# One strided pattern of a dilated attention staged through a GpSimd copy

## The chip, the cores and the metric

The kernel runs on one core of one Trainium2 chip, as a single program. The metric is the device time of one execution in microseconds. Three timed runs of the kernel before gave 2363.19, 2372.0 and 2381.81 us; the median is 2372.0 us.

## The reference

The program is a two-layer decoder trunk over one sequence of 2048 positions of width 1024. The even layer (forgetting attention and gated linear attention) is not touched by the change. The odd layer runs two mixers in parallel on one input projection: a four-head retention and eight heads of dilated attention with 64 channels each. Queries and keys of both are rotated (rope): with the halves x1 and x2 of a head's channels, the result is x1 cos - x2 sin and x2 cos + x1 sin.

The dilated attention of a head is three causal window attentions, whose outputs are mixed by their softmax denominators. Pattern d (d = 1, 4, 16) takes the positions by residue modulo d, cuts every residue class into blocks of 128 and lets a block attend to itself and the block before it. With 2048 positions, dilation 1 has 16 blocks in one class, dilation 4 has 4 classes of 4 blocks, and dilation 16 has 16 classes of one block each, which attend to themselves alone.

```python
qs = to_strided(q)                 # (B, H, dil, nb, 128, dh)
kb = with_prev(to_strided(k))      # the block and the one before it
s = einsum('bhrnqd,bhrnkd->bhrnqk', qs, kb) * dh ** -0.5
p = exp(s - max(s));  den = sum(p)
o = einsum('bhrnqk,bhrnkd->bhrnqd', p, vb) / den;  lse = max(s) + log(den)
# out = sum over the three patterns of softmax(lse) * o
```

## The kernel before, in words

The kernel keeps float32 accuracy with pairs of float16 numbers: a high part and the rest. For each head of the dilated attention, `Heads.tiles` (L402) computes q, k and v for two tiles of 128 positions with 48 matmuls (L183 to L185), rotates q and k (`rope`, L1128, which calls `rotate`, L776: three VectorE multiplications and one GpSimd addition, L785), splits them (L425 to L434) and has them transposed by DMA (L440, SP queue) into `heads.st[h]`, a tile with 128 partitions, three planes (q; k high; k low) and 2048 positions in their natural order.

`dilated` (L869) attends. `groups` (L876) writes v to DRAM and reads it back in two strided orders (L878, L880, L882, all on GpSimd's queue), and forms 12 groups of four blocks each per head: groups 0 to 3 of pattern 0 (dilation 1), 4 to 7 of pattern 1 (dilation 4), 8 to 11 of pattern 2 (dilation 16). `scores` (L897) does the eight matmuls of a group, two for each block (q with k high, q with k low; L911, L912). The moving operand is a slice of `heads.st[h]` with step 1, 4 or 16: 256 columns where there is a block before, else 128; pattern 2 has only 128. VectorE then scales, masks and takes the maximum (L914), ScalarE exponentiates (L918) and makes the float16 high part (L920), VectorE the rest (L921), and two DMA transposes on the SP queue turn both (L922, L923, tile `dl_pt`). `values` (L926) multiplies them by v (L933, L934); ScalarE copies one half out of PSUM to `dl_o1` (L937), and VectorE adds the other half and writes the record `dl_rec` (L940, or L942 and L943). Records of patterns 1 and 2 go to DRAM and come back in natural order (L947, L948, GpSimd's queue). `mixed` (L950) combines the three records of a head.

The order is set in three places. `attend` (L978) lists the groups as 4 to 11 and then 0 to 3; `lagged` with LAG = 2 puts the values of a group behind the scores of the group two later; the last two values and `mixed` of a head go into the steps of the next head (`late`). `periods` (L448) and `merge` (L198) interleave these steps with other work: the tiles of the next head and the projections of the retention and the gate (`Extra.rows`, L240), each a unit with a cost in the plan. Before each step, `merge` issues as much of that work as the step's share of the plan's cost calls for; in the plan, scores cost 0.9 and values 0.7. Last, the framework's scheduler simulates the program and orders each engine's instructions by readiness, so that the order on an engine can differ from the order of the text.

After the eight heads, the retention (L789, which rotates with the same `rotate`) and the output projection of the odd layer (`mix_out`, L311) follow.

Of the kernel before, what the change touches and what calls it, by code (L numbers as in the profile page):

```python
# [7 lines left out]
F32 = mybir.dt.float32  # L8
F16 = mybir.dt.float16
BF16 = mybir.dt.bfloat16  # L10
I32 = mybir.dt.int32
AF = mybir.ActivationFunctionType
# [5 lines left out]
S = 2048  # L18
D = 1024
NT = 16  # L20
# [755 lines left out]
def rotate(co, work, x, cos, lo, hi, name):  # L776

    nc = co.nc
    r = work.tile(list(x.shape), F32, name=name)
    half = "p h (s d) -> p (h s) d" if len(x.shape) == 3 else "p j a (s d) -> p j (a s) d"  # L780
    nc.vector.tensor_mul(r.rearrange(half, s=2), x.rearrange(half, s=2), cos)
    y = work.tile(list(x.shape), F32, name=name + "_y", bufs=1)
    nc.vector.tensor_mul(y[..., 0:32], x[..., 32:64], lo)
    nc.vector.tensor_mul(y[..., 32:64], x[..., 0:32], hi)
    nc.gpsimd.tensor_add(r, r, y)  # L785
    return r


def retention(co, work, qkv_d, gn_w, gn_b, cst, rp):  # L789

    nc = co.nc
# [23 lines left out]
    def step(t, out):  # L815
# [4 lines left out]
        tabs = (rp[:, t, None, a:a + 32].to_broadcast([128, n, 32]) for a, n in ((0, 16), (32, 8), (64, 8)))  # L820
# [48 lines left out]
def dilated(co, work, keep, heads, cst, v_d, rec_d, mix_d):  # L869

    nc = co.nc
    mask = work.tile([128, 256], F32, name="dl_mask", bufs=1)
    nc.sync.dma_start(mask, cst["c_dmask"])
    recs, live = {}, {}

    def groups(h):  # L876
# [15 lines left out]
        for r0 in range(0, 16, 4):  # L892
            out.append((2, [(r, slice(r, S, 16), slice(r, S, 16), [v3[:, r, :]]) for r in range(r0, r0 + 4)]))
        recs[h] = [keep.tile([128, NT, 66], F32, name=f"dl_rec{i}", bufs=2 if i == 1 else 1) for i in range(3)]
        return out

    def scores(h, g, pat, units):  # L897
        rec, st, f = recs[h][pat], heads.st[h], heads.f[h]
        p = co.ps([128, 1024], "big")
# [6 lines left out]
        for n, qs, ks, vs in units:  # L906
            width = 128 * len(vs)
            sp = slice(at, at + width)
            spans.append(sp)
            at += width  # L910
            nc.tensor.matmul(p[:, sp], st[:, 0, qs], st[:, 1, ks], start=True, stop=False)  # L911
            nc.tensor.matmul(p[:, sp], st[:, 0, qs], st[:, 2, ks], start=False, stop=True)  # L912
# [13 lines left out]
    def values(h, g, pat, units):  # L926
# [9 lines left out]
        o1 = work.tile([128, 4, 64], F32, name="dl_o1", bufs=1)  # L936
        nc.scalar.activation(o1, pv[:, :, 0:64], AF.Copy)  # L937
        ns = [un[0] for un in units]
        if ns == sorted(ns):
            nc.vector.tensor_add(rec[:, ns[0]:ns[0] + 4, 0:64], pv[:, :, 64:128], o1)  # L940
        else:
            nc.vector.tensor_add(rec[:, 1:4, 0:64], pv[:, 0:3, 64:128], o1[:, 0:3, :])  # L942
            nc.vector.tensor_add(rec[:, 0:1, 0:64], pv[:, 3:4, 64:128], o1[:, 3:4, :])  # L943
# [34 lines left out]
    def attend(h, ready=None):  # L978
        gs = groups(h)
        order = [4, 5, 6, 7, 8, 9, 10, 11, 0, 1, 2, 3]  # L980
        steps = [(0.9, lambda g=g: scores(h, g, *gs[g]), 0.7, lambda g=g: values(h, g, *gs[g])) for g in order]
        units, wait = lagged(steps, LAG)
        for n, x in enumerate(late):
            units.insert(2 * n + 1, x)
        if ready:
            for i, x in enumerate(ready):
                units.insert(2 * len(late) + 1 + 5 * i, (0.0, x))
        late[:] = wait + [(0.0, lambda: mixed(h))]
        if ready:
            units += late  # L990
        return units
# [4 lines left out]
def decoder(tc, cst, x, norm_even, w_in_even, b_f_even, w_lr_even, b_lr_even, gla_norm_even, w_out_even,  # L996
            norm_odd, w_in_odd, ret_gn_w_odd, ret_gn_b_odd, w_out_odd, final_norm, out):
    nc = tc.nc
    with ExitStack() as ctx:
# [125 lines left out]
        rp = tab[1].tile([128, NT, 96], F32, name="rope")  # L1125
        nc.sync.dma_start(rp, cst["c_rope"])

        def rope(t, q):  # L1128
            tabs = (rp[:, t:t + 2, None, a:a + 32].to_broadcast([128, 2, n, 32])
                    for a, n in ((0, 4), (32, 2), (64, 2)))  # L1130
            return rotate(co, pre[1], q, *tabs, "dl_r")
# [53 lines left out]
def constants():  # L1185
# [17 lines left out]
    rope = np.concatenate([cos, -sin, sin], axis=1)  # L1203
    c["c_rope"] = rope.reshape(NT, 128, 96).transpose(1, 0, 2)
# [34 lines left out]
```

## Time and profile before

| | us |
|---|---|
| median of three runs (lowest, highest) | 2372.0 (2363.19, 2381.81) |
| the profiled execution, its own time | 2365.02 |
| its span, from the first instruction to the last | 2362.9 |
| TensorE matmuls busy | 2177.7 (92%) |
| VectorE busy | 1563.6 (66%) |
| ScalarE busy | 1123.3 (48%) |
| GpSimd busy | 520.9 (22%) |

The mean granted TensorE clock is 0.968 of full speed. Times in the trace are counted from the start of the span. The eight dilated heads run from about 1258 us (the first L911) to about 2064 us; before that lies the even layer, after it the retention and the last projection. PE is TensorE's matmul side, PEld its weight load, DVE VectorE, ACT ScalarE, POOL GpSimd, SP or SPq the queue of SyncE that issues the DMA transposes. Matmuls are pipelined: the time of one matmul in a row includes its way through the array, and the pace is read from the distance between the starts of neighbours.

### The profile page before, as it was taken

The page shows a single profiled execution, that of the slowest core. Times are in us where ns is not written, and L with a number is a line of the kernel's source. Part 1 is how long each engine was busy: PE and PEld are TensorE (multiplying, and loading weights), DVE is VectorE, ACT ScalarE, POOL GpSimd, SP SyncE. Part 2 cuts the span into 40 slices and gives each one's busy share as a digit, 9 for nine tenths or more (in the row PEclk, how much of TensorE's full clock was granted, in tenths as well). Part 3 has the DMA queues.
Part 4 walks back from the last instruction along what each step waited for, and adds up shares of the span by engine and source line. Part 5 has one row for each costly group of instructions (what it writes and reads, how often), then busy time and mean ns, then how long its engine had stood idle before and what let it go on. Part 6 is the DMA issues. An engine that isn't in the chain of part 4 may idle for free.

```text
span 2362.9 us, 51635 instructions
## 1 busy us (share of the span) xinstructions
PE 2177.7 (92%) x20020; PEld 1693.0 (72%) x20020; DVE 1563.6 (66%) x4878; ACT 1123.3 (48%) x2582; POOL 520.9 (22%) x638
## 2 busy tenths in 40 slices
PE   4978899998999999899999999999998899889998
PEld 3767787676688878654449988888887787755554
DVE  6556667575686667566557676757575757778764
ACT  5545455454554556344444554545454545533322
POOL 0021221211212111111112122231322122244431
PEclk7999999999999999999999999999999999989999
DMA  8658897988888858877876688786786668866553
GB/s 192 136 112 149 149 166 147 172 161 154 158 160 157 162 133 186 217 207 203 218 164 141 143 151 159 139 145 136 158 144 127 152 113 168 181 200 191 165 170 107
DMA packets 823606, 377.69 MB, mean 160 GB/s; under 512 B 726192, under 2 KB 782400, under 8 KB 823104
## 3 DMA queue, kind: packets, MB, share of 16 engines
q1 hardware_dynamic: 725936, 255.09, 55.9%
q0 software_dynamic: 23584, 82.33, 12.1%
q10 hardware_dynamic: 73840, 36.97, 6.4%
q8 instruction: 157, 2.57, 0.4%
q14 instruction: 89, 0.73, 0.1%
HBM read 135.40 MB, written 73.73 MB: 89 GB/s over the span
## 4 chain that ended last, share of the span: by engine, by line
PE 52%; DMA 21%; DVE 13%; issue 6%; ACT 5%; SPq 2%; POOL 1%; ACTq 0%; POOLq 0%; DVEq 0%
PE dn L183 9%; PE dn L185 9%; PE dn L184 9%; DMA dl_pt<-dl_pl 4%; DMA fx_tl<-fx_pl 4%; PE dn L354 3%; PE dn L356 3%; PE dn L355 3%; DMA o_gate<-gate_d 2%; PE big L911 2%; PE big L912 2%; PE aux L554 2%; PE big L522 2%; PE big L523 2%; DMA gl_x<-glq_d 1%
## 5 line engine op out<-in xcount | busy, mean ns | idle before, releaser
L183 PE MATMUL dn<-w,uh 128*128 128x192 f16 (+1 forms) x3840 | 1003.4, 261 | 14.7 <-DVE x_out L250 4.0
L184 PE MATMUL dn<-w,uh 128*128 128x192 f16 (+1 forms) x3840 | 1002.9, 261 | 0.0
L185 PE MATMUL dn<-w,ul 128*128 128x192 f16 (+1 forms) x3840 | 1002.3, 261 | 0.6 <-DMA ul<-u_lo 0.6
L183 PEld LDWEIGHTS <-uh 128*128 128x128 f16 x3968 | 391.6, 99 | 39.8 <-ACT uh L122 5.5
L184 PEld LDWEIGHTS <-uh 128*128 128x128 f16 x3968 | 390.6, 99 | 38.4 <-issue 11.0
L185 PEld LDWEIGHTS <-ul 128*128 128x128 f16 x3968 | 390.1, 99 | 28.8 <-DMA ul<-u_lo 2.8
L535 ACT ACTIVATE fx_s<-fx_s,fx_nm 128x1152 f32<-128x1152 f32 (+15 forms) x128 | 152.7, 1194 | 173.9 <-DVE fx_nm L533 170.8
L918 ACT ACTIVATE dl_s<-dl_s,dl_m 128x256 f32<-128x256 f32 (+1 forms) x384 | 172.7, 451 | 124.9 <-DVE dl_m L917 108.6
L540 DVE TENSOR_TENSOR fx_pl<-fx_s,fx_ph 128x2176 f16<-128x2176 f32 x64 | 155.2, 2424 | 93.5 <-DMA fx_tl<-fx_pl 59.2
L914 DVE CUSTOM_DVE_ANT_0 dl_s<-big,dl_mask,hd_f 128x256 f32<-128x256 f32 (+1 forms) x384 | 141.8, 421 | 52.9 <-PE big L912 51.7
L79 POOL TENSOR_TENSOR rs_r<-rs_v,mhalf 128x1 f32<-128x1 f32 (+2 forms) x96 | 68.1, 714 | 363.5 <-DVE rs_v L76 341.8
L527 DVE CUSTOM_DVE_ANT_0 fx_s<-big,cb,hd_f 128x1024 f32<-128x1024 f32 (+7 forms) x128 | 133.8, 1046 | 19.1 <-PE big L523 8.7
L921 DVE TENSOR_TENSOR dl_pl<-dl_s,dl_ph 128x512 f16<-128x512 f32 (+2 forms) x96 | 101.9, 1064 | 66.1 <-ACT dl_ph L920 38.3
L539 ACT ACTIVATE fx_ph<-fx_s 128x2176 f16<-128x2176 f32 x64 | 128.8, 2013 | 34.6 <-DMA fx_th<-fx_ph 31.1
L522 PE MATMUL big<-head 128*128 128x512 f16 (+3 forms) x320 | 112.9, 353 | 31.0 <-DVE fx_m L527 30.9
L84 ACT ACTIVATE w<-w_raw,w_gs 128x256 f16<-128x256 f32 (+2 forms) x296 | 113.7, 466 | 36.8 <-DVE w_gs L164 33.2
L911 PE MATMUL big<-head 128*128 128x256 f16 (+1 forms) x384 | 129.6, 355 | 0.9 <-DVE dl_rec L914 0.8
L912 PE MATMUL big<-head 128*128 128x256 f16 (+1 forms) x384 | 129.7, 357 | 0.0
L85 DVE SCALAR_TENSOR_TENSOR w<-w_raw,w_gs,w 128x256 f16<-128x256 f32 (+2 forms) x296 | 123.3, 469 | 8.4 <-ACT w L84 8.2
L555 PE MATMUL aux<-head,fx_tl 128*128 128x64 f16 x1088 | 102.3, 194 | 22.3 <-DMA fx_tl<-fx_pl 22.2
L566 POOL TENSOR_TENSOR fx_o<-fx_o 128x64 f32<-128x64 f32 x128 | 43.9, 362 | 343.1 <-DVE fx_o L560 212.3
L554 PE MATMUL aux<-head,fx_th 128*128 128x128 f16 x1088 | 107.2, 222 | 7.9 <-DMA fx_th<-fx_ph 7.9
(242 smaller groups left out, 4355.2 us busy)
## 6 DMA issues: line engine op xcount, KB each, us to landing
gate_d<-x_out POOLq DMA_DIRECT2D x64, 256.0 KB, 3.8
o_gate<-gate_d SPq DMA_DIRECT2D x32, 512.0 KB, 4.5
rec_d<-dl_rec POOLq DMA_DIRECT2D x16, 528.0 KB, 4.8
dl_rec<-rec_d POOLq DMA_DIRECT2D x16, 528.0 KB, 6.3
x_h<-in_x_dram SPq DMA_DIRECT2D x16, 512.0 KB, 4.8
cb<-cum_d SPq DMA_DIRECT2D x16, 512.0 KB, 9.7
o_mix<-mix_d SPq DMA_DIRECT2D x32, 256.0 KB, 2.8
o_h<-in_x_dram SPq DMA_DIRECT2D x16, 512.0 KB, 4.5
```

The source lines that it names most:

```text
L183: nc.tensor.matmul(out, uh[:, k, xs], wh[:, k, c0:c1], start=k == 0, stop=False)
L184: nc.tensor.matmul(out, uh[:, k, xs], wl[:, k, c0:c1], start=False, stop=False)
L185: self.last = nc.tensor.matmul(out, ul[:, k, xs], wh[:, k, c0:c1], start=False, stop=k == KT - 1)
L522: nc.tensor.matmul(p[:, k0:k1], q, st[:, ks, 1, 0:kn], start=True, stop=False)
L527: nc.vector.tensor_tensor_reduce(out=x[:, at + c * 1024:at + c * 1024 + wide], in0=p[:, :wide], in1=cb[c][:, :wide], scale=f[:, 0:1], scal ...
L535: nc.scalar.activation(x[:, sp], x[:, sp], AF.Exp, bias=nm[:, part:part + 1], accum_out=nm[:, 2 + part:3 + part])
L540: nc.vector.tensor_sub(pl, x[:, 0:W], ph)
L554: nc.tensor.matmul(pv[:, part, :], th[:, at, :], v[:, k, :], start=k == 0, stop=False)
L911: nc.tensor.matmul(p[:, sp], st[:, 0, qs], st[:, 1, ks], start=True, stop=False)
L912: nc.tensor.matmul(p[:, sp], st[:, 0, qs], st[:, 2, ks], start=False, stop=True)
L914: nc.vector.tensor_tensor_reduce(out=raw[:, sp], in0=p[:, sp], in1=mask[:, 256 - 128 * len(vs):], scale=f[:, 0:1], scalar=-3.0e38, op0=OP. ...
L918: nc.scalar.activation(raw[:, sp], raw[:, sp], AF.Exp, bias=m[:, i:i + 1], accum_out=rec[:, n, 65:66])
```

## The change

Four things change.

The operands of pattern 2 are copied. `stage(h, g)` lets GpSimd copy the 3 x 4 x 128 float16 values per partition that group g of pattern 2 needs from `heads.st[h]` (step 16 positions) into a contiguous tile `dl_g` with a single buffer. Group 8 is staged at the start of the scores of group 4, each next one right behind the matmuls of the group before it. The matmuls of pattern 2 read `dl_g`; those of patterns 0 and 1 read as before.

The groups are reordered to 4, 5, 8, 6, 9, 7, 10, 0, 11, 1, 2, 3, and the plan's costs become 1.05 and 0.84 (scores and values of patterns 0 and 1), 0.55 and 0.44 (pattern 2).

`values` no longer uses `dl_o1`: ScalarE writes into the record, and VectorE adds to it in place.

The rotary table holds cos and sin instead of cos, -sin and sin (64 columns instead of 96), and `rotate` replaces its one GpSimd addition by a subtraction on one half and an addition on the other, each of half the size.

```diff
-def rotate(co, work, x, cos, lo, hi, name):
+def rotate(co, work, x, cos, sin, name):
...
-    nc.vector.tensor_mul(y[..., 0:32], x[..., 32:64], lo)
-    nc.vector.tensor_mul(y[..., 32:64], x[..., 0:32], hi)
-    nc.gpsimd.tensor_add(r, r, y)
+    nc.vector.tensor_mul(y[..., 0:32], x[..., 32:64], sin)
+    nc.vector.tensor_mul(y[..., 32:64], x[..., 0:32], sin)
+    nc.gpsimd.tensor_sub(r[..., 0:32], r[..., 0:32], y[..., 0:32])
+    nc.gpsimd.tensor_add(r[..., 32:64], r[..., 32:64], y[..., 32:64])
...
-            out.append((2, [(r, slice(r, S, 16), slice(r, S, 16), [v3[:, r, :]]) for r in range(r0, r0 + 4)]))
+            out.append((2, [(r, None, None, [v3[:, r, :]]) for r in range(r0, r0 + 4)]))
...
+    def stage(h, g):
+
+        if g < 12:
+            staged[h, g] = work.tile([128, 3, 4, 128], F16, name="dl_g", bufs=1)
+            nc.gpsimd.tensor_copy(staged[h, g], heads.st[h].rearrange("p s (i r) -> p s r i", r=16)[:, :, 4 * (g - 8):4 * (g - 7), :])
+
     def scores(h, g, pat, units):
         rec, st, f = recs[h][pat], heads.st[h], heads.f[h]
+        if g == 4:
+            stage(h, 8)
...
-            nc.tensor.matmul(p[:, sp], st[:, 0, qs], st[:, 1, ks], start=True, stop=False)
-            nc.tensor.matmul(p[:, sp], st[:, 0, qs], st[:, 2, ks], start=False, stop=True)
+            q, kh, kl = ((st[:, 0, qs], st[:, 1, ks], st[:, 2, ks]) if pat < 2 else
+                         (staged[h, g][:, s, n % 4, :] for s in range(3)))
+            nc.tensor.matmul(p[:, sp], q, kh, start=True, stop=False)
+            nc.tensor.matmul(p[:, sp], q, kl, start=False, stop=True)
+        if pat == 2:
+            stage(h, g + 1)
...
-        o1 = work.tile([128, 4, 64], F32, name="dl_o1", bufs=1)
-        nc.scalar.activation(o1, pv[:, :, 0:64], AF.Copy)
         ns = [un[0] for un in units]
-        if ns == sorted(ns):
-            nc.vector.tensor_add(rec[:, ns[0]:ns[0] + 4, 0:64], pv[:, :, 64:128], o1)
-        else:
-            nc.vector.tensor_add(rec[:, 1:4, 0:64], pv[:, 0:3, 64:128], o1[:, 0:3, :])
-            nc.vector.tensor_add(rec[:, 0:1, 0:64], pv[:, 3:4, 64:128], o1[:, 3:4, :])
+        for a, b in ((0, 4),) if ns == sorted(ns) else ((0, 3), (3, 4)):
+            to = rec[:, ns[a]:ns[b - 1] + 1, 0:64]
+            nc.scalar.activation(to, pv[:, a:b, 0:64], AF.Copy)
+            nc.vector.tensor_add(to, pv[:, a:b, 64:128], to)
...
-        order = [4, 5, 6, 7, 8, 9, 10, 11, 0, 1, 2, 3]
-        steps = [(0.9, lambda g=g: scores(h, g, *gs[g]), 0.7, lambda g=g: values(h, g, *gs[g])) for g in order]
+        order = [4, 5, 8, 6, 9, 7, 10, 0, 11, 1, 2, 3]
+        steps = [(c, lambda g=g: scores(h, g, *gs[g]), 0.8 * c, lambda g=g: values(h, g, *gs[g]))
+                 for c, g in ((0.55 if g > 7 else 1.05, g) for g in order)]
...
-        rp = tab[1].tile([128, NT, 96], F32, name="rope")
+        rp = tab[1].tile([128, NT, 64], F32, name="rope")
...
-    rope = np.concatenate([cos, -sin, sin], axis=1)
-    c["c_rope"] = rope.reshape(NT, 128, 96).transpose(1, 0, 2)
+    rope = np.concatenate([cos, sin], axis=1)
+    c["c_rope"] = rope.reshape(NT, 128, 64).transpose(1, 0, 2)
```

## Rows read from the trace of the kernel before

**Rows 1.** The page's part 1: busy us, share of the span, instructions.

```profile
PE 2177.7 (92%) x20020; PEld 1693.0 (72%) x20020; DVE 1563.6 (66%) x4878; ACT 1123.3 (48%) x2582; POOL 520.9 (22%) x638
```

**Rows 2.** Stretches, dilated heads second: length, engines' busy us, clock, DMA share, GB/s.

```profile
0.00:1258.00 1258.00, 1136.04 (x10720) 863.30 (x10721) 807.38 (x2038) 611.17 (x1123) 210.44 (x329) 0.97 0.80 167
1258.00:2064.00 806.00, 763.86 (x7811) 675.58 (x7810) 544.90 (x2250) 417.53 (x1282) 194.82 (x209) 0.98 0.74 146
2064.00:2362.00 298.00, 277.81 (x1493) 154.13 (x1490) 211.31 (x591) 94.60 (x179) 115.59 (x102) 0.94 0.56 169
```

**Rows 3.** Waits of PE, 1258 to 2064 us: total us, times, longest.

```profile
PE aux L934 <- DMA dl_pt<-dl_pl: 29.3, 10, 6.8
PE aux L933 <- DMA dl_pt<-dl_ph: 9.5, 5, 4.9
```

**Rows 4.** Timeline of PE in a group of pattern 2: start, us, what.

```profile
1393.78 0.43 PE L912 MATMUL big<-head 128*128 128x128 f16 x1
1394.02 0.43 PE L911 MATMUL big<-head 128*128 128x128 f16 x1
1394.26 0.43 PE L912 MATMUL big<-head 128*128 128x128 f16 x1
```

**Rows 5.** Timeline of PE in a group of pattern 0, then values.

```profile
1438.44 0.27 PE L912 MATMUL big<-head 128*128 128x256 f16 x1
1438.55 0.22 PE L911 MATMUL big<-head 128*128 128x128 f16 x1
1438.60 0.22 PE L912 MATMUL big<-head 128*128 128x128 f16 x1
1438.66 0.22 PE L933 MATMUL aux<-dl_v,dl_pt 128*128 128x128 f16 x1
1438.72 0.19 PE L934 MATMUL aux<-dl_v,dl_pt 128*128 128x64 f16 x1
1438.74 0.22 PE L933 MATMUL aux<-dl_v,dl_pt 128*128 128x128 f16 x1
```

**Rows 6.** Groups on GpSimd, shapes apart, whole span: busy us, mean ns, idle before.

```profile
L785 POOL TENSOR_TENSOR dl_r<-dl_r,dl_r_y 128x256 f32<-128x256 f32 x64 | 50.9, 795 | 202.0 <-DVE dl_r_y L784 131.4 <-DVE w_tot L159 20.5 <-DVE w_am L153 18.6
L971 POOL TENSOR_TENSOR dl_rec<-dl_rec,dl_es 128x1024 f32<-128x1024 f32 x24 | 46.5, 1954 | 37.4 <-DVE dl_es L968 22.0 <-DVE dl_m L917 6.5 <-ACT dl_s L918 5.6
L501 POOL TENSOR_SCALAR cb<-cb,hd_f 128x1024 f32<-128x1024 f32 x16 | 45.5, 2843 | 81.0 <-DMA cb<-cum_d 81.0
```

**Rows 7.** Timeline of all engines at a head's start.

```profile
1364.46 5.89 SPq L440 DMA_TRANSPOSE head<-qk_x  x3
...
1370.39 0.28 PE L911 MATMUL big<-head 128*128 128x128 f16 x1
...
1371.45 0.55 POOL L882 DMA_DIRECT2D dl_v<-v_d  x1
```

**Rows 8.** DMA issues: size where shown, median us to landing.

```profile
head<-qk_x SPq DMA_TRANSPOSE x128, 4.2
```

**Rows 9.** Timeline of all engines while a head is mixed.

```profile
1899.00 5.62 POOL L971 TENSOR_TENSOR dl_rec<-dl_rec,dl_es 128x1024 f32<-128x1024 f32 x3 [7.01 <-DVE dl_es L968]
...
1902.80 2.91 DVE L972 TENSOR_TENSOR dl_rec<-dl_rec,dl_rec 128x1024 f32<-128x1024 f32 x1 [2.98 <-POOL dl_rec L971]
```

**Rows 10.** Groups on VectorE, shapes apart, 1258 to 2064 us.

```profile
L921 DVE TENSOR_TENSOR dl_pl<-dl_s,dl_ph 128x1024 f16<-128x1024 f32 x48 | 62.5, 1305 | 28.9 <-DMA dl_pt<-dl_pl 14.6 <-ACT dl_ph L920 12.8 <-ACT w L84 1.3
L972 DVE TENSOR_TENSOR dl_rec<-dl_rec,dl_rec 128x1024 f32<-128x1024 f32 x7 | 10.2, 1463 | 8.7 <-POOL dl_rec L971 8.7
```

**Rows 11.** Single lines of VectorE: ns min/median/max, first and last start.

```profile
L921 DVE TENSOR_TENSOR dl_pl<-dl_s,dl_ph x96: 678/1211/2795, 1275.5 to 2043.0; 128x1024 f16<-128x1024 f32 x48, 128x512 f16<-128x512 f32 x40, 128x896 f16<-128x896 f32 x8
L972 DVE TENSOR_TENSOR dl_rec<-dl_rec,dl_rec x8: 1214/1227/2908, 1385.5 to 2070.7; 128x1024 f32<-128x1024 f32 x8
```

**Rows 12.** Groups of the values, shapes apart, 1258 to 2064 us.

```profile
L937 ACT ACTIVATE dl_o<-aux 128x256 f32<-128x256 f32 x96 | 36.0, 376 | 69.5 <-PE aux L934 62.3 <-DVE dl_rec L940 6.3 <-DVE dl_rec L914 0.5
L940 DVE TENSOR_TENSOR dl_rec<-aux,dl_o 128x256 f32<-128x256 f32 x88 | 36.7, 417 | 20.6 <-ACT dl_o L937 20.5
```

More of the change, by code (lines that the diff above doesn't have):

```diff
@@ L819, in step @@
         v = z[:, 512:1024].rearrange("p (h n) -> p h n", n=128)
-        tabs = (rp[:, t, None, a:a + 32].to_broadcast([128, n, 32]) for a, n in ((0, 16), (32, 8), (64, 8)))
+        tabs = (rp[:, t, None, a:a + 32].to_broadcast([128, n, 32]) for a, n in ((0, 16), (32, 8)))
         r = rotate(co, work, z[:, 0:512].rearrange("p (h d) -> p h d", d=64), *tabs, "rt_r")
@@ L873, in dilated @@
     nc.sync.dma_start(mask, cst["c_dmask"])
-    recs, live = {}, {}
+    recs, live, staged = {}, {}, {}
     def groups(h):
@@ L1129, in rope @@
             tabs = (rp[:, t:t + 2, None, a:a + 32].to_broadcast([128, 2, n, 32])
-                    for a, n in ((0, 4), (32, 2), (64, 2)))
+                    for a, n in ((0, 4), (32, 2)))
             return rotate(co, pre[1], q, *tabs, "dl_r")
```

## The prediction

> **What bounds the kernel now.** I began with the page's busy shares: TensorE is busy for 92% of the span, VectorE for 66%, ScalarE for 48%, GpSimd for 22% [rows 1]. An average over the whole program says little about one stage, so I cut it at the dilated heads. Their stretch is 806 us long; TensorE is busy for 763.9 of it (95%) at a granted clock of 0.98, which is the higher of its two levels nearly all the time, VectorE for 544.9 (68%), ScalarE for 417.5 (52%), GpSimd for 194.8 (24%) [rows 2]. The reader is to see that TensorE alone sets the length there, and that GpSimd has the most room. TensorE's 42.1 us of idle time have nearly one cause: values that wait for their transposed probabilities, 29.3 + 9.5 us in 15 waits [rows 3]. In eight heads that is about two waits among twelve groups.
>
> **What the copies buy.** The pace of a matmul is the distance from its start to its neighbour's. In a group of pattern 2 the starts lie 0.24 us apart, for 128 columns read at a step of 16 positions [rows 4]. In a group of pattern 0, whose keys are contiguous, a matmul of 256 columns takes 0.11 us and one of 128 columns 0.05 to 0.06 us [rows 5]. The same 128 columns thus cost four times as much when they are read with a step. Staged operands are contiguous for q, k high and k low alike, so I take 0.057 us. Eight heads times four groups times eight matmuls are 256 matmuls; 256 x (0.24 - 0.057) = 46.8 us less on the engine that sets the end. Pattern 1 is not staged and keeps its pace. The bounds of this term are nothing (the pace came from something else than the step) and 256 x 0.19 = 48.6 us.
>
> **What the copies cost.** A copy moves 3 x 4 x 128 = 1536 values per partition; there are 32. No copy on GpSimd stands in the trace. The nearest row with one tensor operand is L501, 2.843 us for 1024 values, 2.8 ns each; the two-operand L971 takes 1.954 us for 1024, 1.9 ns each [rows 6]. That makes 2.9 to 4.3 us for a copy. I take 4.3, since L501 has the copy's single input; both rows read densely, so the step could make it longer, and TensorE's ratio of 0.24 to 0.057 gives the far end, 18 us. 32 x 4.3 = 138 us of GpSimd.
>
> [...]
>
> **Does TensorE wait for a copy?** The tile has one buffer, so the copy for the next narrow group starts after the matmuls of the one before. The plan's cost of a head is 12 steps: 1.8 x (8 x 1.05 + 4 x 0.55) = 19.08. TensorE's work of a head is 763.9 / 8 = 95 us, of which its own scores and values are some 25 us and the filling work 70 us (my count: 32 matmuls of 0.11, 32 of about 0.23, 32 of 0.24, 75 pairs of values of 0.085). Between two narrow scores lie two values, one wide score and the narrow one itself, 2.88 to 3.28 of 19.08, thus 10.6 to 12 us of filling and 2 to 3 us of its own: 12.5 to 15 us. A copy of 4.3 us leaves 8 us for delays in GpSimd's queue. The first copy of a head is tighter. It needs all transposes of q and k; in the second head these are issued from 1364.46 to 1370.35 us and land 4.2 us later, at about 1374.5, and on GpSimd it stands behind v's way through DRAM, whose last issue ends at 1372.0 [rows 7, 8]. Started at 1374.5, it ends near 1379. The head's first scores start at 1370.39 and its third group, now group 8, comes some 15 us later, near 1385: 6 us of slack. Behind a waiting copy stand GpSimd's stores of the projections, the rotations of the next head and the record transfers; they delay ScalarE's x_out buffers first. I allow 1 us for each of the eight first copies, 8 us (bounds 0 and 8 x 6).
>
> **What the copies do to VectorE.** While L971 ran from 1899.00 to 1904.62, L972 started at 1902.80 and took 2.91 us instead of its median of 1.227, ending 1.09 us after L971 did [rows 9, 11]. So a VectorE operation with two SBUF operands is held while GpSimd works. Over the stretch L921's wide form averages 1305 ns against a median of 1211, 4.5 us in 48, and L972 1463 against 1227, 1.7 us in 7 [rows 10, 11]; that is 6 us for 97 us of GpSimd arithmetic [rows 6]. If all of VectorE's 545 us stretched as these 73 us do, it would be 47 us. The added GpSimd work (138 us, and 26 us for the rotations below) then holds VectorE for 10 to 79 us; I take 25, near the low end, since most of its other operations read PSUM or one operand. VectorE has 261 us of idle time here, so only that part counts that makes a transpose late where TensorE waits already, 2 groups of 12: 4 us.
>
> [...]
>
> **The rest.** Each rotation's addition becomes two halves. From 795 ns for 256 and 1954 ns for 1024 values [rows 6] a half of 128 takes about 0.6 us, so two add 0.4 us: 26 us on GpSimd for 64 rotations, between VectorE and ScalarE work for the next head, hidden by TensorE's filling; without that cover 26 us more, and in the retention 16 x 0.4 = 6 us, also beside TensorE. The smaller table is one load, and nothing waits for it. Dropping `dl_o1` leaves 96 copies of 376 ns and 88 additions of 417 ns [rows 12] as they are, splits eight copies (at most 8 x 0.4 = 3 us of ScalarE, idle for 48%) and frees one buffer; nothing on TensorE.
>
> **The order.** A value group has as cover what the plan puts between its scores and itself: before, 3.2 of 19.2 everywhere (16.7%); after, 15.1% for five groups of a head, and 17 to 20% for the others, those at the head's end among them. For the three wide ones of the five that is 1.1 us less of the filling, 3 x 8 x 1.1 = 26 us at worst; at best most of the 38.8 us of late transposes go. A narrow group between wide ones also gives VectorE, ScalarE and the transposes an easier stretch. I take nothing, with both ends kept.
>
> **Sum.** -46.8 + 8 + 4 = -35 us. The profiled execution took 2365.0 us (span 2362.9 and 2.1 around it); 2330 follows for one like it. The median of the three runs is 7 us higher, so I forecast 2337 us.
>
> **The rivals.**
> - *The order and the copies together give more*: the copies cost nothing and 15 us of late transposes go: 2365 - 47 - 15 = 2303, with the 7 us 2310. For it: the mixing of narrow and wide groups. Against: the waits are few and may sit where a head's weights are prepared. 8%.
> - *The gain is given back at the transposes*: VectorE, held by copies, delivers L921 late, values wait, TensorE idles instead of reading with a step. It takes 47 / 32 = 1.5 us for each copy to cancel all: 2365 to 2372. For it: L972's row, and less TensorE work to hide the same chain. Against: VectorE's 32% idle. A part of this gives 2350 to 2372. 20%.
> - *The step is not what makes pattern 2 slow*: then nothing is bought, and the 12 us are lost: 2384. Against: 256 contiguous columns take less than 128 stepped ones. 4%.
> - *Slower, because the copy is long*: a GpSimd read with a step pays like TensorE's. At 18 us a copy no longer fits the 12.5 to 15 us between narrow groups; TensorE waits some 4 us in each of three gaps and 14 - 6 = 8 us at the first copy of every head, 20 x 8 = 160 us, less 47: 2485. It decides once a copy takes more than about 12 us, less what stands before it in the queue. Against: GpSimd's rows lie far below this per value. Anything slower by over 1%: 8%.
>
> **The numbers.** The forecast itself has 60%, and its own range is 2315 to 2350. With the rivals the range is 2303 to 2378: below lies part of the first, above the third and the slow one, together under 2 in 10. One per cent of 2372, about what a measurement can tell, is 24 us: faster than 2348 are the first rival and nearly all of the forecast, 66%; within 1% the second, the third and an edge of the forecast, 26%; slower than 2396, 8%.
>
> **What would show it.** After the change L911 and L912 of pattern 2 should stand 0.05 to 0.06 us apart, and TensorE's busy time in the dilated stretch should fall by about 47 us. A copy should take near 4 us, and TensorE's waits for GpSimd at L911 should sum to 10 us or so. L921's mean should rise above 1305 ns, and the waits at L933 and L934 should stay near 39 us. The prediction is wrong if the copy takes over 10 us, if waits for `dl_g` or `dl_pt` take up the 47 us, or if the pace of pattern 2 stays at 0.24 us.

## The result, and the profile after

The changed kernel took 2395.1 us (median of 4 runs, 2382.7 to 2402.3) beside 2367.6 us of the kernel before on the same chip: ratio 1.013, 95% interval 1.0084 to 1.0175. It is slower by some 31 us; the forecast was 35 us faster. The profiled execution, the longest of the four, took 2402.3 us (span 2400.5), against 2365.0.

Lines have moved: the scores' matmuls are L922 and L923 (before L911, L912), the subtraction L934 (L921), the probabilities' transposes L935 and L936, the values L946 and L947 (L933, L934), the mixing L981 and L982 (L971, L972). The copy is L902.

The page's part 1 of the changed kernel, to be laid beside [rows 1]:

```profile
PE 2162.5 (90%) x20020; PEld 1686.2 (70%) x20020; DVE 1604.9 (67%) x4878; ACT 1118.4 (47%) x2590; POOL 652.6 (27%) x750
```

Its stretches, with the columns of [rows 2]: the dilated heads, then the rest.

```profile
1252.00:2091.00 839.00, 744.82 (x7916) 670.00 (x7915) 591.13 (x2240) 414.86 (x1293) 309.27 (x302) 0.95 0.74 140
2091.00:2400.00 309.00, 277.59 (x1388) 150.31 (x1386) 205.98 (x603) 92.19 (x177) 129.88 (x118) 0.88 0.54 163
```

The dilated stretch grew from 806 to 839 us although TensorE is busy for 19 us less (the forecast looked for some 47 less; 7916 matmuls in place of 7811 fall into the stretch, and the clock is lower). Its idle time there rose from 42.1 to 94.2 us, and the granted clock fell from 0.98 to 0.95: of the 806 single microseconds of the stretch before, 769 read 1.00 and 26 read 0.50; of the 839 here, 744 and 69. TensorE's waits in that stretch, which answer to [rows 3]:

```profile
PE aux L946 <- DMA dl_pt<-dl_ph: 43.9, 11, 8.0
PE aux L947 <- DMA dl_pt<-dl_pl: 26.2, 18, 3.7
PE dn L183 <- DVE head L430: 7.5, 3, 5.3
PE aux L157 <- DVE w_am L155: 5.9, 1, 5.9
```

The waits for transposed probabilities went from 38.8 us in 15 to 70.1 us in 29; those for the high part went from 9.5 to 43.9. TensorE has no wait for `dl_g` in this trace. Where the forecast looked for the gain, it is there: in TensorE's timeline a group of pattern 2 runs at the pace of [rows 5], no longer at that of [rows 4].

```profile
1492.09 0.22 PE L922 MATMUL big<-dl_g 128*128 128x128 f16 x1
1492.15 0.22 PE L923 MATMUL big<-dl_g 128*128 128x128 f16 x1
1492.21 0.22 PE L922 MATMUL big<-dl_g 128*128 128x128 f16 x1
```

GpSimd's groups over the whole span (busy us, mean ns, idle before), beside [rows 6]:

```profile
L902 POOL COPY dl_g<-head 128x1536 f16<-128x1536 f16 x32 | 97.1, 3035 | 98.8 <-PE big L923 49.2 <-DMA head<-qk_x 44.1 <-DVE dl_m L930 4.1
L785 POOL TENSOR_TENSOR dl_r<-dl_r,dl_r_y 128x128 f32<-128x128 f32 x64 | 41.7, 652 | 128.2 <-DVE dl_r_y L783 116.0 <-ACT dl_ph L933 4.6 <-ACT dl_s L931 3.3
L786 POOL TENSOR_TENSOR dl_r<-dl_r,dl_r_y 128x128 f32<-128x128 f32 x64 | 34.2, 534 | 0.0
```

A copy takes 3.0 us, and the queue stands 98.8 us in all in front of copies that can't start yet. A seam between two heads shows where the time goes. Lines of the timelines of SP's queue, GpSimd and TensorE there, in order of time:

```profile
1461.22 6.29 SPq L440 DMA_TRANSPOSE head<-qk_x  x3
1467.68 2.56 SPq L935 DMA_TRANSPOSE dl_pt<-dl_ph  x1
1468.29 0.79 POOL L881 DMA_DIRECT2D dl_v<-v_d  x1 [1.55 <-DMA v_d<-head]
1469.08 0.55 POOL L883 DMA_DIRECT2D dl_v<-v_d  x1
1470.30 8.87 SPq L936 DMA_TRANSPOSE dl_pt<-dl_pl  x1
1481.04 2.92 POOL L902 COPY dl_g<-head 128x1536 f16<-128x1536 f16 x1 [11.41 <-DMA head<-qk_x]
1483.93 0.45 POOL L785 TENSOR_TENSOR dl_r<-dl_r,dl_r_y 128x128 f32<-128x128 f32 x1
1483.95 0.29 PE L946 MATMUL aux<-head,dl_pt 128*128 128x128 f16 x1 [7.64 <-DMA dl_pt<-dl_ph]
```

The two reads of V (512 KB each) are issued between the last group's two transposes; the second transpose then occupies SP's queue for 8.87 us, and TensorE stands still for 7.64. Five other waits of 3.8 to 8.0 us for `dl_ph` lie elsewhere in the stretch.

### The profile page after: what moved, and what is told of

Same layout as the page of the kernel before. It is cut to its first block, busy times and chain, and to the rows that moved or that the text cites. A ratio compares the mean times of both kernels' runs of the same rounds, so it can differ in the third digit from the quotient of the medians.

```text
span 2400.5 us, 51773 instructions
## 1 busy us (share of the span) xinstructions
PE 2162.5 (90%) x20020; PEld 1686.2 (70%) x20020; DVE 1604.9 (67%) x4878; ACT 1118.4 (47%) x2590; POOL 652.6 (27%) x750
## 4 chain that ended last, share of the span: by engine, by line
PE 46%; DMA 23%; DVE 14%; issue 7%; ACT 6%; SPq 2%; POOL 1%; ACTq 0%; DVEq 0%; POOLq 0%
PE dn L183 8%; PE dn L185 7%; PE dn L184 7%; DMA dl_pt<-dl_pl 4%; DMA fx_tl<-fx_pl 4%; PE dn L354 3%; PE dn L356 3%; PE dn L355 3%; DMA dl_pt<-dl_ph 2%; DMA w_raw<-in_w_in_odd_dram 2%; DMA o_gate<-gate_d 2%; PE aux L554 2%; PE big L522 2%; PE big L523 1%; DMA gl_x<-glq_d 1%
## 5 line engine op out<-in xcount | busy, mean ns | idle before, releaser
L183 PE MATMUL dn<-w,uh 128*128 128x192 f16 (+1 forms) x3840 | 1007.8, 262 | 26.8 <-DVE head L430 9.1
L183 PEld LDWEIGHTS <-uh 128*128 128x128 f16 x3968 | 393.7, 100 | 43.5 <-ACT uh L122 5.5
L934 DVE TENSOR_TENSOR dl_pl<-dl_s,dl_ph 128x512 f16<-128x512 f32 (+1 forms) x96 | 110.3, 1149 | 62.9 <-ACT dl_ph L933 41.9
L152 DVE TENSOR_REDUCE w_am<-w_raw 128x8 f32<-128x2048 f32 (+2 forms) x41 | 83.1, 2028 | 63.9 <-DMA w_raw<-in_w_in_odd_dram 29.2
L902 POOL COPY dl_g<-head 128x1536 f16<-128x1536 f16 x32 | 97.1, 3035 | 98.8 <-PE big L923 49.2
```

The costliest lines, as they stand in the source:

```text
L183: nc.tensor.matmul(out, uh[:, k, xs], wh[:, k, c0:c1], start=k == 0, stop=False)
```

## The experiments

All ratios are to the kernel before on the same chip, with 95% intervals; "us" beside one is the ratio's difference from 1 times some 2364 us. The "old order" is that of the kernel before, costs included; where a kernel has it, its diff is not shown again:

```
-order = [4, 5, 8, 6, 9, 7, 10, 0, 11, 1, 2, 3]
-steps = [(c, ..., 0.8 * c, ...) for c, g in ((0.55 if g > 7 else 1.05, g) for g in order)]
+order = [4, 5, 6, 7, 8, 9, 10, 11, 0, 1, 2, 3]
+steps = [(0.9, ..., 0.7, ...) for g in order]
```

### The parts one by one

**e_pace**, the kernel before with contiguous operands and nothing else:

```
-(r, slice(r, S, 16), slice(r, S, 16), [v3[:, r, :]])
+(r, slice(128 * r, 128 * r + 128), slice(128 * r, 128 * r + 128), [v3[:, r, :]])
```

> The kernel before, whose third pattern reads 128 contiguous positions in place of those 16 apart: other operands, so its output is not the reference's, and no copies. All theories take the pace as real: 256 matmuls at 0.055 instead of 0.24 us, 47 us less work on TensorE. If TensorE alone bounds the stretch, 2368 - 47 + 5 = 2320 to 2335 us. If the chain behind the scores bounds it as well (shorter TensorE work hides less of it), only a part comes through: 2335 to 2360 us.

Measured 0.9858 (0.9820 to 0.9897), 34 us faster. The step is what made pattern 2 slow.

**e_rotate**, the kernel before with the rotation's halves and the one sine alone (the diff of `rotate` and of the table in the change).

> The kernel before with the rotation's GpSimd addition in two halves and the smaller table, nothing else. [...] Theory B would allow a little, up to 10 us slower, since the rotations stand between VectorE and ScalarE: 2368 to 2378 us.

Measured 1.000 (0.9968 to 1.0031). Nothing, as predicted.

**e_order**, the kernel before with the new order and costs alone (the diff above, reversed).

> The kernel before with the new order and plan costs alone (no copies, old rotation, dl_o1 kept). Theory A, the order: in the changed kernel the third pattern's records now go through DRAM at a head's start, together with v's two strided reads and the last transposes of q and k, and the transposes that the values wait for land late. Then this kernel has the same long waits (7 to 8 us at a head's start) and is slower than before by 20 to 50 us: 2390 to 2420 us. Theory B, the copy at the head of GpSimd's queue: a copy that waits for the last transposes holds the rotations behind it, ScalarE waits for these. Then this kernel is within 10 us of before: 2358 to 2378 us.

Measured 1.0177 (1.0121 to 1.0232), 42 us slower with no copy in it. The order alone makes the kernel slow. The first line of its page and two lines of TensorE's waits in the dilated stretch (1254 to 2107 us):

```profile
PE 2201.5 (91%) x20020; PEld 1707.3 (71%) x20020; DVE 1561.7 (65%) x4878; ACT 1120.4 (46%) x2582; POOL 529.7 (22%) x638
PE aux L933 <- DMA dl_pt<-dl_ph: 30.1, 6, 13.4
PE big L912 <- DMA head<-qk_x: 14.4, 3, 6.9
```

The profiled span is 49.6 us longer than before. Beside [rows 1], the same 20020 matmuls keep TensorE busy for 23.8 us more, at a mean granted clock of 0.950 in place of 0.968; the other 25.8 us are idle time. The scores wait there for the head's own transposes too, 14.4 us in place of 0.2. So only about half of the order's price in this execution stands in a list of waits.

**e_order_old**, the changed kernel with the old order.

> The changed kernel with the old order and the old plan costs (copies, halved rotation, record written in place). Theory A: the gain of the copies shows, 25 to 40 us faster than before: 2328 to 2343 us. Theory B: group 8's copy still stands in GpSimd's queue at the head's start and waits for the last transposes, so most of the loss stays: 2370 to 2400 us. [...]

Measured 0.9968 (0.9938 to 0.9999), 8 us faster (the interval is 0 to 15). So two things went wrong: the order costs 1.013 - 0.9968, 38 us, and without it most of the 34 us of the pace are still missing.

### What in the order

**e_mix11**: group 11 ahead of group 0, `order = [4, 5, 8, 6, 9, 7, 10, 11, 0, 1, 2, 3]`. **e_mix_costs**: the new order with the old costs (0.9 and 0.7).

> The changed kernel with one place of its order put back: group 11 ahead of group 0, so that the third pattern's records are stored and fetched back one group earlier, as in the kernel before (whose order has 11 eight places in). Costs and all else as changed. Theory P (pile-up at the seam between two heads: the late round trip of the records, the next head's reads of V and its first transposes meet in the DMA engines): most of the 35 us that the order costs on top of the copies come back, 2365 to 2375 us, TensorE's waits for dl_pt 45 us or less (70 after). Rival C (the costs told to the planner make the loss, the order of groups does not): nothing changes, 2390 to 2400. Rival I (the interleaving itself, the third pattern's short groups early in the head, makes the loss): also 2385 to 2400; C and I are told apart by the next run.

> The changed kernel with the new order of groups but the old costs told to the planner (0.9 for scores and 0.7 for values, whatever the pattern). Rival C (costs): back to the time of the changed kernel with old order and costs, 2355 to 2370 us. Theories P and I (it is where the groups stand): 2385 to 2400 us, with waits of 4 us and more for dl_pt at most heads' starts, as after.

Measured 1.0108 (1.0055 to 1.0161) and 1.0138 (1.0069 to 1.0206). The planner's costs are not it. The late round trip of the records is worth 5 us (1.013 - 1.0108), which these intervals can't tell from nothing; theory P wanted 2365 to 2375 us and got 2387. It fell.

**e_third**: `order = [4, 5, 6, 8, 7, 9, 10, 11, 0, 1, 2, 3]`, still with the new costs. The first group of pattern 2 comes fourth instead of third, the second sixth instead of fifth.

> The changed kernel with the order 4, 5, 6, 8, 7, 9, 10, 11, 0, 1, 2, 3: the groups of the third pattern still among the others, but the first of them in fourth place instead of third, and group 11 ahead of group 0. Rival L (what counts is that a group that needs every position of the head comes in third place; in the old order the first such group is the fourth, 7): the loss of the order goes, 2355 to 2368 us. Rival I (short groups among long ones leave less time between a group's scores and its values): 2378 to 2392 us as with 8 in third place (2387). Theory S: near 2380, since the seam's transposes and reads are those of the run with group 11 put back.

Measured 1.0007 (0.9971 to 1.0043): 24 us back from e_mix11, though the groups are still mixed. So most of the loss hangs on what stands third and fifth. TensorE's waits for `dl_pt` in the dilated stretch are 57.5 us in e_mix11 and 32.3 in e_third. One seam of each shows a difference. First a seam of e_mix11 (timelines of SP, GpSimd and TensorE):

```profile
1563.59 8.04 SPq L440 DMA_TRANSPOSE head<-qk_x  x3
1568.97 0.79 POOL L881 DMA_DIRECT2D dl_v<-v_d  x1 [4.78 <-PE dn L185]
1569.76 0.55 POOL L883 DMA_DIRECT2D dl_v<-v_d  x1
1571.79 5.19 SPq L935 DMA_TRANSPOSE dl_pt<-dl_ph  x1
1577.03 12.60 SPq L936 DMA_TRANSPOSE dl_pt<-dl_pl  x1
1590.04 2.95 POOL L902 COPY dl_g<-head 128x1536 f16<-128x1536 f16 x1 [18.84 <-DMA head<-qk_x]
1590.71 0.29 PE L946 MATMUL aux<-head,dl_pt 128*128 128x128 f16 x1 [13.21 <-DMA dl_pt<-dl_ph]
1590.80 0.42 PE L183 MATMUL dn<-w,uh 128*128 128x256 f16 x1
1591.01 0.42 PE L184 MATMUL dn<-w,uh 128*128 128x256 f16 x1
```

Then the same seam of e_third:

```profile
1547.00 7.32 SPq L440 DMA_TRANSPOSE head<-qk_x  x3
1554.48 1.24 SPq L935 DMA_TRANSPOSE dl_pt<-dl_ph  x1
1555.76 2.44 SPq L936 DMA_TRANSPOSE dl_pt<-dl_pl  x1
1558.82 0.81 POOL L881 DMA_DIRECT2D dl_v<-v_d  x1
1559.62 0.55 POOL L883 DMA_DIRECT2D dl_v<-v_d  x1
1561.01 2.97 POOL L902 COPY dl_g<-head 128x1536 f16<-128x1536 f16 x1
```

In e_mix11 V's reads are ahead of the last group's transposes, which take SP 5.2 and 12.6 us to issue; in e_third the transposes are first, take 1.2 and 2.4 us, and TensorE has no wait there. Stretches of both seams (columns as in [rows 2]), e_mix11:

```profile
1571.00:1577.00 6.00, 6.00 (x60) 4.91 (x58) 1.81 (x15) 3.02 (x12) 0.20 (x1) 1.00 1.27 171
1577.00:1584.00 7.00, 0.50 (x3) 0.00 (x0) 3.55 (x20) 2.64 (x10) 0.00 (x0) 0.81 1.30 83
1584.00:1591.00 7.00, 0.29 (x2) 0.24 (x3) 0.00 (x0) 0.25 (x1) 0.96 (x1) 0.50 1.28 114
```

and e_third:

```profile
1553.00:1560.00 7.00, 7.00 (x69) 5.82 (x68) 4.66 (x29) 3.26 (x12) 4.89 (x4) 1.00 1.17 168
1560.00:1567.00 7.00, 7.00 (x70) 5.98 (x69) 5.17 (x16) 1.88 (x7) 4.66 (x5) 1.00 0.86 225
```

The reader is to see two costs in e_mix11: 13 us of idle TensorE, during which the granted clock falls from 1.00 to 0.50, and slow matmuls behind the wait: those of 256 columns start 0.21 us apart there (1590.80 and 1591.01). How long that lasts can be read in the changed kernel's trace, behind its wait of 7.64 us, which ends at 1483.95: the clock reads 1.00 up to 1477 us and 0.50 from 1478 to 1487; the matmuls of 256 columns start 0.21 us apart from 1485.72 to 1487.64, 3.7 us behind the wait's end, and 0.11 apart from 1487.83.

**e_no_v** and **e_old_no_v**: are V's reads the cause? Heads 1 to 7 keep the first head's V (14 reads of 512 KB fewer), in the new order and in the old.

```
-v2 = work.tile(...); nc.gpsimd.dma_start(v2, v_d[h]...)   # and v3
+if h == 0: (the same)                                     # and v3
```

> The changed kernel (new order) in which only the first head reads its rearranged V back from DRAM; heads 1 to 7 use the first head's tiles. [...] Theory S (seam: V's two reads are issued just behind the last group's transposes, and these land 11 to 21 us after their issue while both share the DMA engines): the waits of 4 us and more for dl_pt at the heads' starts go, dl_pt below 30 us in all (68 after), and the time falls by 30 us or more, to 2365 us or less. Rival L (the third group in the order is a group of the third pattern, which reads every 16th position and so needs the last tile of the head one group earlier; the projection's last tiles, not V, are late): at most 10 to 15 us, 2380 to 2390 us.

> The control of the run before: the changed kernel with old order and costs, and the same 14 reads of V left out. Theory S: V's reads cost the old order little, since its last transposes are ahead of them: 2350 to 2361 us, so that the two orders come within 10 us of each other without V's reads. Rival L: both orders gain alike, 5 to 15 us each, and stay 25 us or more apart.

Measured 1.0031 (0.9995 to 1.0066) and 0.9876 (0.9841 to 0.9911). The reads cost some 22 us, but in both orders: without them the orders are still 37 us apart (38 with them). V's reads stand beside the long waits of the seams shown, but they are not the reason for the difference between the orders. Theory S fell.

**e_seven**: is it that a group that needs every position of the head comes third? Group 7 is long, and needs the last 512 positions too. The records of pattern 1 leave with group 6, now the later one.

```
-order = [4, 5, 6, 7, 8, 9, 10, 11, 0, 1, 2, 3]
+order = [4, 5, 7, 6, 8, 9, 10, 11, 0, 1, 2, 3]
-if pat and g % 4 == 3:
+if g in (6, 11):
```

> The changed kernel with the old costs and the order 4, 5, 7, 6, 8, 9, 10, 11, 0, 1, 2, 3: the old order with group 7 in third place, a long group (1024 columns) of the second pattern that needs the head's last 512 positions; its records leave when group 6, now the later, is done. Rival L (every position is needed one group earlier): 20 to 30 us over the old order, 2378 to 2392 us, ratio 1.005 to 1.011. Rival I (a short group gives less cover): as the old order, 2352 to 2365 us, ratio 0.995 to 1.000.

Measured 0.9971 (0.9940 to 1.0002), as the old order. Rival L fell as well. What is left of the named ones is I in a narrower form: short groups in third and fifth place, between the long groups of pattern 1, cost 24 us, while in fourth and sixth place they cost little (1.0007 against 0.9968, intervals that overlap).

### Where the copies' price comes from

**e_late_stage**: the copies issued later in the program.

```
+if g in (4, 6, 7, 8):          # at the start of values(h, g)
+    stage(h, 8 if g == 4 else g + 3)
```

> The changed kernel with old order and costs, in which a copy is issued later, on GpSimd still: that of group 8 with the values of group 4 instead of the scores of group 4, those of groups 9, 10, 11 with the values of groups 6, 7 and 8 instead of directly behind the matmuls that read the tile. [...] Rival Q (GpSimd's queue stands behind a copy that waits 80 us in all for the matmuls and for the head's transposes, the rotation behind it): these waits fall below 30 us and most of the 27 us come back, 2335 to 2348 us. [...] If TensorE begins to wait for dl_g itself, that wait stands in its list, a few us for each copy, and the time goes above 2365.

Measured 1.0008 (0.9975 to 1.0041). Inconclusive: the instructions are put in order by the scheduler afterwards, and GpSimd still stood 70.5 us in front of its copies (78.8 in e_order_old), so the wait was hardly taken away.

**e_twice** (old order, every copy made twice) and **e_act_copy** (old order, the copies on ScalarE).

```
+for _ in range(2): nc.gpsimd.tensor_copy(staged[h, g], ...)     # e_twice
+nc.scalar.activation(staged[h, g], ..., AF.Copy)                # e_act_copy
```

> The changed kernel in the old order and costs, with each of the 32 copies made twice in a row (the second writes the same values again). 97 us more of GpSimd work in the stretch. Theory V (VectorE is stretched in proportion to GpSimd's copying): VectorE's busy time in the stretch rises by some 30 us more and the time by 20 to 30 us, 2380 to 2390 us. Rival Q (the queue behind the copy that waits): each head's first rotation and records are held 3 us more, 8 heads, at most 5 to 15 us, with VectorE's durations hardly longer than with one copy. If the copy's price is neither: 2361 us as before.

> The changed kernel in the old order and costs, with the 32 copies made by ScalarE in place of GpSimd. Theory V (the copies' price is the stretch of VectorE's instructions beside GpSimd's copies): VectorE's 1024-form subtraction falls back from 1421 to about 1305 ns, VectorE's busy time in the stretch by some 30 us, and most of the 27 us come back: 2335 to 2348 us, unless ScalarE's own queue becomes late. Rival Q (the copies' price is GpSimd's queue: the copy that waits for the head's transposes holds the rotation and the records behind it): these too are gone from GpSimd's queue, so 2335 to 2348 us too, but the exponentials now stand behind the copy on ScalarE: waits for dl_ph grow. Rival N (the price is the wait of the third pattern's matmuls for any copy): 2355 to 2370 us as with GpSimd. [...]

Measured 1.0380 (1.0318 to 1.0443), so some 100 us of second copies cost 97 us, three to five times V's figure. But VectorE's busy time rose by 68 us too (1604.0 in e_order_old, 1671.7 in e_twice, by their pages), not by V's 30: what fell is a stretch in proportion, not the stretch as a cause. With the copies on ScalarE the kernel measured 0.9957 (0.9930 to 0.9984), which can't be told from 0.9968 on GpSimd: VectorE is not stretched there (1560.3), and the time is not won. This doesn't say what the stretch costs on GpSimd, since copies on ScalarE can have a price of their own, in its queue.

**e_pace_old** and **e_unread** (both old order): the third pattern reads contiguous positions of the head, without copies, and with copies that nobody reads.

```
+(st[:, s, 128 * n:128 * n + 128] for s in range(3))    # in place of staged[h, g]
+if g < 0:                                              # stage(), in e_pace_old alone
```

> The changed kernel with old order and costs, without the copies: the third pattern's matmuls read 128 contiguous positions of the head in place of the 16-step ones (so they compute with other positions). If the copies swallow the gain: 2325 to 2340 us, as with the contiguous operands alone in the kernel before (ratio 0.986). If another part of the change does (the eviction that writes into the record itself and makes VectorE add in place, the rotation in halves): 2350 to 2361, and the copies are innocent.

> As the run before, but with the 32 copies made on GpSimd and read by nobody: the matmuls read 128 contiguous positions of the head. No matmul waits for a copy, and no copy waits for a matmul. [...] Rival D (the dependence: the copy waits 54 us for the matmuls before it, and with it what stands behind it on GpSimd): 2330 to 2345 us.

Measured 0.9821 (0.9785 to 0.9856) and 0.9992 (0.9966 to 1.0019). This is the clearest pair: 32 copies that wait for no matmul, and for which no matmul waits, cost 40 us. Rival D fell. Of the 51 us between the two profiled spans 26.5 are TensorE's busy time (2132.0 and 2158.5 us for the same 20020 matmuls, at a mean clock of 0.967 and 0.957), the rest idle time. Groups over the whole span in e_pace_old (busy us, mean ns):

```profile
L934 DVE TENSOR_TENSOR dl_pl<-dl_s,dl_ph 128x1024 f16<-128x1024 f32 x48 | 62.1, 1297 | 28.9 <-ACT dl_ph L933 19.4 <-DMA dl_pt<-dl_pl 9.5
L428 DVE SCALAR_TENSOR_TENSOR qk_x<-dl_r,qk_x 128x128 f16<-128x128 f32 x128 | 31.1, 283 | 19.3 <-ACT qk_x L425 19.3
L428 DVE SCALAR_TENSOR_TENSOR qk_x<-dn,qk_x 128x128 f16<-128x128 f32 x128 | 30.8, 282 | 6.7 <-ACT head L426 6.7
```

in e_unread:

```profile
L902 POOL COPY dl_g<-head 128x1536 f16<-128x1536 f16 x32 | 100.1, 3130 | 28.8 <-DMA head<-qk_x 19.8 <-issue 8.9
L934 DVE TENSOR_TENSOR dl_pl<-dl_s,dl_ph 128x1024 f16<-128x1024 f32 x48 | 84.5, 1762 | 36.4 <-ACT dl_ph L933 29.8 <-DMA dl_pt<-dl_pl 6.5
L428 DVE SCALAR_TENSOR_TENSOR qk_x<-dl_r,qk_x 128x128 f16<-128x128 f32 x128 | 49.6, 428 | 13.9 <-ACT qk_x L425 13.9
L428 DVE SCALAR_TENSOR_TENSOR qk_x<-dn,qk_x 128x128 f16<-128x128 f32 x128 | 30.8, 282 | 6.6 <-ACT head L426 6.6
```

and in e_act_copy:

```profile
L902 ACT ACTIVATE dl_g<-head 128x1536 f16<-128x1536 f16 x32 | 96.2, 3007 | 40.8 <-DMA head<-qk_x 22.5 <-PE big L923 14.2 <-DVE dl_rec L927 4.0
L934 DVE TENSOR_TENSOR dl_pl<-dl_s,dl_ph 128x1024 f16<-128x1024 f32 x48 | 60.3, 1258 | 33.1 <-ACT dl_ph L933 30.8 <-ACT w L84 1.3 <-DMA dl_pt<-dl_pl 0.7
L428 DVE SCALAR_TENSOR_TENSOR qk_x<-dl_r,qk_x 128x128 f16<-128x128 f32 x128 | 34.6, 310 | 10.3 <-ACT qk_x L425 10.0
```

On GpSimd, 100 us of copies put 22 us on the wide subtractions and 19 us on L428, on the way from scores to transposes and from a projection to the head's transposes. The form of L428 that reads `dn` from PSUM, with one operand in SBUF, stays at 282 ns. On ScalarE the copies put nothing on the subtractions and 3.5 us on L428; there they are 96 us in the queue in which the exponentials stand. The price is much the same, 32 us (0.9957 - 0.9821).

**e_k_only** and **e_act_k**: only K's two parts, the moving operands, are copied; Q is read at the step of 16.

```
-[128, 3, 4, 128] ... [:, :, 4 * (g - 8):4 * (g - 7), :]
+[128, 2, 4, 128] ... [:, 1:3, 4 * (g - 8):4 * (g - 7), :]
-(staged[h, g][:, s, n % 4, :] for s in range(3))
+(st[:, 0, n::16], *(staged[h, g][:, s, n % 4, :] for s in range(2)))
```

> The changed kernel with old order and costs, in which only the moving operands (K's two parts) are copied by GpSimd, 1024 values in place of 1536, about 2.0 in place of 3.0 us each; Q stays the stationary operand read at every 16th position, whose load took 0.15 us in place of 0.10 in the kernel before. If the copies' price goes with their length (a third of 20 to 27 us comes back, and the loads hide behind the matmuls): 2345 to 2356 us. If the strided load sets the pace at 0.10 us and more per matmul (128 pairs, 256 matmuls, 8 us and more for each 0.03 us): 2356 to 2366.

> The same two thirds of the copies, on ScalarE. From the full copies on ScalarE (0.9957 of the kernel before) a third of the copies' price back: 0.990 to 0.995, about 2340 to 2352 us; the fastest of the versions that compute the reference, if the strided loads of Q stay hidden. Otherwise as the full copies on ScalarE or slower.

Measured 0.9867 (0.9820 to 0.9913) and 0.9889 (0.9841 to 0.9938): 31 and 26 us faster than the kernel before. On GpSimd a third of the copying less gave back 24 us of 35. TensorE's timeline in e_k_only shows that the weights' step costs the pace nothing:

```profile
1385.97 0.23 PE L923 MATMUL big<-dl_g,head 128*128 128x128 f16 x1
1386.03 0.22 PE L922 MATMUL big<-dl_g,head 128*128 128x128 f16 x1
1386.09 0.23 PE L923 MATMUL big<-dl_g,head 128*128 128x128 f16 x1
```

**e_k_halves**: the same, each copy in two halves in three buffers of two sequences.

```
+for r in (4 * (g - 8), 4 * (g - 8) + 2):
+    x = work.tile([128, 2, 2, 128], F16, name="dl_g", bufs=3)
+    nc.gpsimd.tensor_copy(x, ...[:, 1:3, r:r + 2, :])
```

> The kernel with old order and costs in which GpSimd copies K's two parts alone (0.987), with each copy made in two halves of two sequences, 512 values each, in three buffers, so that the next group's first half needn't wait for the matmuls. If the wait for the matmuls (43 us of GpSimd's idle time) is part of what is left of the price: 2318 to 2328 us, ratio 0.981 to 0.985. If the work itself is (unread copies cost 40 us without any wait for matmuls): as with whole copies, 2326 to 2338, or a few us more for 32 more instructions.

Measured 0.9856 (0.9815 to 0.9896), 2321.0 us beside 2362.2. It beats both kernels, the changed one by 2.7%; whether the halves add to e_k_only can't be told from these intervals. They didn't do what they were meant to: GpSimd stood 57.5 us in front of its copies for TensorE's matmuls, 42.5 in e_k_only.

Over the runs with GpSimd's copies in the old order, the price goes with what VectorE's busy time gains over e_pace_old (1555.5 us, whole span): 28 us and a price of 8 in e_k_halves, 33 and 11 in e_k_only, 49 and 35 in e_order_old, 53 and 40 in e_unread, 116 and 132 in e_twice. GpSimd's own work grows along with it, so this doesn't prove which of the two is paid for. On ScalarE VectorE gains less than 5 us, and the prices are 32 (e_act_copy) and 16 (e_act_k).

## Why the prediction was wrong

Against the sum, as ratios worked into us: the pace and the small parts gave 42 us (e_pace_old; predicted 46.8), the copies took 35 (0.9968 - 0.9821; predicted 8 + 4), and the order took 38 (predicted 0). That is 31 us slower; the three steps lead from one kernel to the next, so they add up by construction.

- **The pace: right.** 0.057 us, as forecast; alone it is worth 34 us, and 42 beside the rest of the change (intervals that overlap).
- **The copy's length: right in its bounds.** 3.0 us, between 2.9 and 4.3; the far end of 18 us, and with it the slow rival, did not come. What the step adds to a copy is not shown: a copy that reads densely stands in no run here.
- **TensorE waits for copies 8 us: too much, and the wrong place.** There is no wait for `dl_g`. The first copy of a head waited for the head's transposes as foreseen (up to 11.4 us here, 44.1 in all), but it was GpSimd and its rotations that stood behind it: in the seam shown a rotation (L785) starts right behind the copy, and ScalarE's waits for rotations rose from 23.2 to 46.3 us (24.9 in the old order).
- **The order: "I take nothing". This is the step that failed.** It cost 38 us in the changed kernel and 42 alone, beyond the upper bound of 26. The bound counted only the filling work between a group's scores and its values. It didn't look at the seams between heads, where the traces show the long waits for `dl_pt` (70.1 us in all in place of 38.8), and it gave waits no price in clock: in e_order 24 of 50 us are the same matmuls running longer at a lower clock (0.950 against 0.968). Why this order brings the waits about is not shown: without V's reads the orders stay 37 us apart.
- **VectorE's hold: "only that part counts that makes a transpose late": 4 us, where the copies' whole price is 35.** This is the second step that failed, and without the order's 38 us it would have left about 2360 us, inside the whole range of 2303 to 2378 but above the forecast's own. The stretch itself was in the bounds: VectorE's busy time grew from 544.9 to 591.1, 46 us of the 10 to 79. (The median of 1211 ns that the working sets beside the wide form's mean is that of all 96 subtractions; the wide form's own is 1224, which changes its 4.5 us to 3.9.) But that the slack of 261 us would swallow all but a sixth is not borne out: on GpSimd the price goes with the stretch. From e_pace_old to e_unread the wide subtraction, with two SBUF operands, went from 1297 to 1762 ns and L428 on `dl_r` from 283 to 428, while L428 on `dn` stayed at 282. That doesn't explain the copies' price on ScalarE, which is nearly as high (32 us) with the subtraction at 1258 ns; a busy share of 24% or 52% is no measure of slack on the path from scores to transposes.
- **The rest: right.** Halves of 0.65 and 0.53 us, and no effect of the rotation on the time; dropping `dl_o1` was not run by itself.

Of the rivals, the second (the gain given back at the transposes, 2350 to 2372) has the time of the changed kernel in the old order (about 2360), but that is in part luck: its waits for `dl_pt` are 32.8 us there, fewer than the 38.8 before. TensorE waits for VectorE's work on the projections instead (12.9 us at L183 for L430), and its mean clock over the span is 0.956 against 0.968. The slower side, which had 8%, came by a mechanism that no rival named. Of the signs of being wrong that the prediction gave, the waits for `dl_pt` were the one that came: 31 us more.

What stays open: why short groups in third and fifth place make the waits at the seams longer, when V's reads, the planner's costs and the need of the whole head in third place have each been taken out, and the records' place gave 5 us that can't be told from nothing; how much of the price on GpSimd is VectorE's stretch and how much GpSimd's queue; and through which wait the copies on ScalarE cost their 32 us.

## What to carry to other kernels

When a change moves the order of work, don't take it as free because the covers look alike: run the order by itself (here it cost 42 us), and look at what the seams do to the DMA queues. A gather that lifts one engine's pace was paid here on either engine that made it (35 us on GpSimd, 32 on ScalarE), even where nobody waited for it (40 us in e_unread); copy only the operand whose step hurts (K's two parts here: a price of 11 us in e_k_only). Price a long wait of TensorE at its length and at the lower clock that follows it (here 7.64 us, then 3.7 us at a clock of 0.50).

## What the hardware showed beyond that

- The stationary operand's step doesn't slow a matmul here: with Q still at a step of 16 (weight loads of 0.15 us instead of 0.10) and K contiguous, the pace was 0.06 us; with K at that step too it was 0.24.
- The price of the copies rises steeply: 66 us of GpSimd's copying cost some 11 us (0.9867 - 0.9821, intervals that overlap), 97 us cost 35, and 196 us cost 132, with VectorE's busy time up by 33, 49 and 116 us.
- GpSimd and ScalarE make this gather in the same time: 3035 and 3007 ns for 1536 values.
- The issue of a transpose can stand long on SP's queue: 12.6 us for one in e_mix11's seam, with V's reads issued just before, against 1.2 to 2.4 in the seam of e_third where the transposes came first. V's reads are not shown to be the reason; elsewhere e_third has an issue of 8.9 us as well.
